# Side transfers of weight sums on ScalarE's queue, seven raw buffers for output tiles, and packed rows of scale and bias in a fox/RWKV-7 layer

## The chip, the cores and the metric

The kernel runs on one core of a Trainium2 chip. The time is device microseconds of one execution, and the numbers compared are medians of several. The engines of the core are TensorE (PE in profiles, its weight loads PEld), VectorE (DVE), ScalarE (ACT), GpSimd (POOL) and SyncE (SP). Each runs its own list of instructions in order; semaphores make one wait for another. A DMA is issued by an instruction on an engine's queue and is carried out by 16 DMA engines.

## The reference, cut to what matters

```python
proj = einsum('bsd,dc->bsc', x, w_in)            # 256 x 4096 by 4096 x 16592
fox_out  = fox_attention(q, k, v, log_sigmoid(f + f_bias))        # 16 heads of 128
rwkv_out = groupnorm(rwkv7_scan(r, decay, k, v, -kk, kk * a)) + bonus   # 32 heads of 64
h   = concat(fox_out, rwkv_out) * silu(z)
out = einsum('bsc,cd->bsd', h, w_out)            # 256 x 4096 by 4096 x 4096
x   = layernorm(ALPHA * x + out, ln_gain, ln_bias)
```

## The kernel before, in words

All products are made in float32r: a weight tile is split into a rounded half (ScalarE, L153) and the rest (VectorE, L154), and TensorE sums three products of halves. A raw weight tile is 128 x 1024 float32 (two rows of 128 inputs by 512 columns, 512 KB), loaded by SyncE in `load` (L252) into a ring of four buffers. `fetch` (L258) keeps up to three loads ahead of the split, and `weights` (L276) up to three split tiles ahead of TensorE. A full tile is used in 12 matmuls of 512 columns.

The program has two halves. **The projection** goes over eight pairs of head groups (n), four blocks (b) of 512 columns each and 16 tiles (q) a block. After every second group of three matmuls it calls `slot` (L212), which lets each of a list of generators (`sides`) issue its next step; `wait(n)` in a generator passes n slots. The generators do everything that is not projection: attention, the RWKV-7 scan in chunks, transposes through DRAM (`bt`, `vt`), gates, and the weight sums.

**The output projection** has eight blocks of 512 columns. For blocks 3/4 and 5/6 and eight of the 16 tiles (`FEW`), a scheme of the Strassen kind saves products. It needs four combinations of four weight tiles b11, b12, b21, b22, two from each block of the pair. They are made ahead, during the projection, by `weight_sums` (L833): two loads of 512 KB from `w_o` into `ts`, four subtractions on GpSimd (L842), one store of 1 MB to DRAM (`td`). There is one `ts` buffer, and 16 sums in all. In the output stage a tile of FEW is a group of four jobs: e1 (a tile of w_o, 6 matmuls), e2 (half a tile, 3), e3 and e4 (halves of `td`, 6 each). The other tiles are plain jobs ("n") of 12. `plan` (L221 to 229) writes the order of the jobs down; `stream` and `jobs` follow it, so the loads stand in SyncE's queue in this order too. Between jobs, `drain` issues pending VectorE work (`todo`) of blocks done before.

`load_tok` (L932) loads the residual and the rows of scale and bias for a block: it makes three-term splits of them in six partitions of `rows` (128 x 4096, zero elsewhere). At the end `moments` (L1248) computes the layer norm's factors; they are written into six columns of a zeroed 128 x 128 tile, transposed by TensorE, and multiplied with `rows` (L1311, L1348), which gives the outer products of the norm with scale and bias.

Names in profiles: `w` and `wo` are raw tiles, with h and l behind them the halves; `e` the raw tiles of e1 to e4; `acc`, `oacc`, `p` PSUM accumulators; `ts` and `td` the sums.

Of the kernel before, what the change touches and what calls it, by code (L numbers as in the profile page):

```python
# [92 lines left out]
def layer(ctx: ExitStack, tc: tile.TileContext, xt, xtok, w_main, w_lora, w_first, muv, w_o, up, par, mulora, fbias, lng, lnb, cst, out):  # L93
# [156 lines left out]
    raws = {}  # L250

    def load():  # L252
        name, src = stream.pop()
        raw = wpool.tile([P, 1024], F32, tag="wr", name=name, bufs=4)
        nc.sync.dma_start(out=raw[:, : src.shape[1] * OB], in_=src.rearrange("p k c -> p (k c)"))
# [577 lines left out]
    def weight_sums():  # L833
        g = nc.gpsimd.tensor_tensor
        for b, q in tds:
            t = rp.tile([P, 4, OB], F32, tag="ts", name=f"ts{b}_{q}")
            for n in range(2):
                issue(t[:, 2 * n : 2 * n + 2], w_o[b + n][:, 2 * q : 2 * q + 2, :])
            yield from wait(6)
            b11, b21, b12, b22 = (t[:, n] for n in range(4))  # L840
            for o, x, y in ((b11, b12, b11), (b12, b22, b12), (b22, b22, b11), (b21, b21, b22)):
                g(o, x, y, ALU.subtract)  # L842
# [89 lines left out]
    def load_tok(b):  # L932
# [5 lines left out]
        rr = rpool.tile([6, OB], F32, tag="rr", name=f"rr{b}")  # L938
        nc.sync.dma_start(out=rr[0:3], in_=lng[:, o].to_broadcast([3, OB]))
        nc.sync.dma_start(out=rr[3:6], in_=lnb[:, o].to_broadcast([3, OB]))  # L940
        rh = rpool.tile([6, OB], F32R, tag="rh", name=f"rh{b}")
        nc.scalar.copy(rh, rr)
        rt_ = rpool.tile([6, OB], F32, tag="rt", name=f"rt{b}")
        nc.vector.tensor_scalar(rt_, rh.bitcast(F32), cs[0:6, C_ROW : C_ROW + 1], None, ALU.mult)
        nc.vector.scalar_tensor_tensor(rows[0:6, o], rr, cs[0:6, C_ROW + 1 : C_ROW + 2], rt_, ALU.mult, ALU.add)
# [220 lines left out]
    whole = len(FEW) * 5 + LEAD  # L1166
    for kind, b, q in plan:
# [51 lines left out]
        if b == 0 and q == KT // 2 - 1:  # L1219
# [5 lines left out]
            rows = rpool.tile([P, D], F32R, name="rows")  # L1225
# [21 lines left out]

    def moments(m):  # L1248
# [6 lines left out]
        nc.gpsimd.memset(z[:, 3:5], 1.0)  # L1255
# [6 lines left out]
        if m:  # L1262
            h = [rpool.tile([P, 1], F32R, name=f"zah{n}") for n in range(2)]
            nc.gpsimd.tensor_copy(h[0], mean)  # L1264
            nc.gpsimd.tensor_copy(za[:, 0:3:2], h[0].bitcast(F32).to_broadcast([P, 2]))
            nc.gpsimd.tensor_tensor(za[:, 1:2], mean, h[0].bitcast(F32), ALU.subtract)
            nc.scalar.copy(h[1], sd)
            nc.scalar.copy(za[:, 3:5], h[1].bitcast(F32).to_broadcast([P, 2]))
            nc.scalar.activation(za[:, 5:6], h[1].bitcast(F32), AF.Identity, scale=-1.0, bias=sd)
# [76 lines left out]
    def other(n):  # L1346
        o = slice(n * OB, (n + 1) * OB)
        nc.tensor.matmul(wps[n], la, rows[:, o], start=False, stop=True)  # L1348
# [64 lines left out]
```

## Time and profile before

| | |
|---|---|
| runs | 1958.45, 1960.71, 1960.96 us; median 1960.71 |
| profiled execution | 1960.14 us, its span 1958.4 us |
| TensorE, VectorE, ScalarE, GpSimd busy | 98%, 76%, 52%, 18% of the span |
| DMA | 466.74 MB, mean 238 GB/s |

The busy share of TensorE counts a matmul from its start to a modelled end, and ends overlap the next start; the distance between starts is the better measure of pace. A row of the table by stages has the stretch, its length, and for each engine its busy time with the number of instructions, then the granted TensorE clock, the share of time in which the DMA engines were busy, and GB/s. "A <- B: t, n, m" in the waits is A waiting for B, t us in total, n times, at most m.

### The profile page before, as it was taken

To read this page: it belongs to the slowest core of one execution; us is meant where nothing else is said; L and a number is where in the kernel's file an instruction comes from. 1 tells how busy PE (TensorE), PEld (TensorE's weight loads), DVE (VectorE), ACT (ScalarE), POOL (GpSimd) and SP (SyncE) were. 2 spreads that over 40 slices of the span, in tenths; PEclk is the share of its full clock that TensorE was granted. 3 is DMA by queue.
4 is the path that set the end of the run, shared out by engine and by line. 5 is a ranking of instruction groups with operands and counts; after the bars stand their busy time and mean duration, and the time that the engine had idled before them with its cause. 6 is when DMAs were issued, how large, how long until landed. Compare 5 with 4: busy or idle time off the path is not lost.

```text
span 1958.4 us, 28349 instructions
## 1 busy us (share of the span) xinstructions
PE 1915.0 (98%) x9745; PEld 1574.4 (80%) x9745; DVE 1484.7 (76%) x2469; ACT 1012.2 (52%) x1581; POOL 361.9 (18%) x530
## 2 busy tenths in 40 slices
PE   9999999999999999999999999999999999998998
PEld 9888787778787888788888888888888878866766
DVE  7688868786878687868776877778677856966667
ACT  6544555455535653555446454645564554554543
POOL 0233223222332142212200220131013001000000
PEclk9999999999999999999999999999999999999999
DMA  9678877886897788777776687677777876777784
GB/s 345 193 249 265 256 229 255 270 250 195 276 278 241 228 284 263 239 215 242 228 224 195 209 243 215 199 224 231 206 218 217 301 221 211 224 255 244 262 263 168
DMA packets 281348, 466.74 MB, mean 238 GB/s; under 512 B 143666, under 2 KB 170948, under 8 KB 279156
## 3 DMA queue, kind: packets, MB, share of 16 engines
q1 hardware_dynamic: 280916, 464.59, 76.3%
q8 instruction: 76, 1.25, 0.3%
q14 instruction: 68, 0.56, 0.1%
q10 hardware_dynamic: 288, 0.34, 0.1%
HBM read 418.43 MB, written 46.42 MB: 237 GB/s over the span
## 4 chain that ended last, share of the span: by engine, by line
PE 81%; DVE 7%; DMA 7%; ACT 2%; SPq 1%; issue 1%; DVEq 0%; ACTq 0%; POOL 0%
PE acc L161 21%; PE acc L159 21%; PE acc L160 20%; PE oacc L963 4%; PE oacc L960 4%; PE oacc L961 4%; DMA e<-td 2%; DMA w<-in_w_main_dram 2%; DMA e<-in_w_o_dram 1%; SPq L318 1%; PE rh L691 1%; PE gp L577 1%; DVE prod L644 1%; PE up L722 1%; PE sp L732 1%
## 5 line engine op out<-in xcount | busy, mean ns | idle before, releaser
L806 POOL COPY pT<-lg 32x96 f32<-32x96 f32 x128 | 58.3, 456 | 419.7 <-DVE lg L802 414.9
L842 POOL TENSOR_TENSOR ts<-ts 128x512 f32<-128x512 f32 x64 | 100.4, 1568 | 182.9 <-DMA ts<-in_w_o_dram 177.6
L614 POOL COPY BKt<-BK 32x192 f32<-32x192 f32 x128 | 73.2, 572 | 60.8 <-DVE BK L611 55.8
L644 DVE TENSOR_TENSOR prod<-Nb,xc 128x8 f32<-128x8 f32 (+30 forms) x248 | 78.1, 315 | 2.9
L647 DVE TENSOR_REDUCE xc<-prod 128x8 f32<-128x16 f32 (+30 forms) x248 | 72.5, 292 | 6.6
L154 DVE TENSOR_TENSOR w_0l<-w,w_0h 128x1024 fp32r<-128x1024 f32 x31 | 37.9, 1222 | 36.5 <-ACT w_0h L153 25.4
L153 ACT CAST w_0h<-w 128x1024 fp32r<-128x1024 f32 x31 | 32.5, 1047 | 55.3 <-DMA w<-in_w_main_dram 41.4
L153 ACT CAST w_6h<-w 128x1024 fp32r<-128x1024 f32 x31 | 32.7, 1055 | 50.0 <-PE acc L160 27.0
L1264 POOL CAST zah<-mv 128x1 fp32r<-128x1 f32 x1 | 0.2, 188 | 305.9 <-DVE mv L1259 305.9
L154 DVE TENSOR_TENSOR w_11l<-w,w_11h 128x1024 fp32r<-128x1024 f32 x31 | 39.8, 1284 | 21.9 <-ACT w_11h L153 11.6
L154 DVE TENSOR_TENSOR w_7l<-w,w_7h 128x1024 fp32r<-128x1024 f32 x31 | 40.4, 1305 | 19.3 <-ACT w_7h L153 8.6
L154 DVE TENSOR_TENSOR w_10l<-w,w_10h 128x1024 fp32r<-128x1024 f32 x31 | 38.8, 1251 | 20.3 <-ACT w_10h L153 12.2
L503 POOL COPY hr<-hr 32x16 f32<-32x16 f32 x64 | 38.4, 600 | 78.6 <-DVE hr L500 76.2
L153 ACT CAST w_8h<-w 128x1024 fp32r<-128x1024 f32 x31 | 32.6, 1051 | 37.5 <-DMA w<-in_w_main_dram 20.6
L161 PE MATMUL acc<-w_11l,x 128*128 128x512 f32 x124 | 47.6, 397 | 4.1 <-DVE w_11l L154 4.1
L154 DVE TENSOR_TENSOR w_8l<-w,w_8h 128x1024 fp32r<-128x1024 f32 x31 | 40.8, 1317 | 14.3 <-ACT w_8h L153 10.5
L787 POOL TENSOR_SCALAR_AFFINE_SELECT nb<-nb 128x128 f32<-128x128 f32 x32 | 22.7, 716 | 153.5 <-DMA nb<-ncd 93.5
L159 PE MATMUL acc<-w_9h,x 128*128 128x512 f32 x124 | 50.1, 404 | 0.8 <-ACT w_9h L153 0.8
L154 DVE TENSOR_TENSOR w_6l<-w,w_6h 128x1024 fp32r<-128x1024 f32 x31 | 38.9, 1254 | 15.6 <-PE acc L161 7.5
L159 PE MATMUL acc<-w_10h,x 128*128 128x512 f32 x124 | 49.6, 400 | 1.0 <-ACT w_10h L153 1.0
L161 PE MATMUL acc<-w_12l,x 128*128 128x512 f32 x124 | 48.1, 392 | 2.2 <-DVE w_12l L154 2.2
L154 DVE TENSOR_TENSOR w_15l<-w,w_15h 128x1024 fp32r<-128x1024 f32 x31 | 38.5, 1242 | 15.3 <-issue 13.1
(1052 smaller groups left out, 6845.8 us busy)
## 6 DMA issues: line engine op xcount, KB each, us to landing
w<-in_w_main_dram SPq DMA_DIRECT2D x496, 512.0 KB
wo<-in_w_o_dram SPq DMA_DIRECT2D x96, 512.0 KB
ts<-in_w_o_dram SPq DMA_DIRECT2D x32, 512.0 KB
td<-ts SPq DMA_DIRECT2D x16, 1024.0 KB
e<-td SPq DMA_DIRECT2D x32, 512.0 KB
bt<-bk SPq DMA_DIRECT2D x88, 128.0 KB
Nb<-nd SPq DMA_DIRECT2D x16, 512.0 KB
e<-in_w_o_dram SPq DMA_DIRECT2D x16, 512.0 KB
```

What stands on the lines that cost most here:

```text
L153: latest[1] = nc.scalar.copy(hi[:, :n], src[:, :n])
L154: latest[0] = nc.vector.tensor_tensor(lo[:, :n], src[:, :n], hi[:, :n].bitcast(F32), ALU.subtract)
L159: nc.tensor.matmul(acc[:, :n], xs[k][:, 0, tt], hi[:, o : o + n], start=(k == 0), stop=False)
L160: nc.tensor.matmul(acc[:, :n], xs[k][:, 1, tt], hi[:, o : o + n], start=False, stop=False)
L161: nc.tensor.matmul(acc[:, :n], xs[k][:, 0, tt], lo[:, o : o + n], start=False, stop=(k == KT - 1))
L614: nc.gpsimd.tensor_copy(BKt[B * b : B * (b + 1), :, :, B * a : B * (a + 1)], BK[B * a : B * (a + 1), :, : NCH - 1, B * b : B * (b + 1)])
L644: first = nc.vector.tensor_tensor(prod[:, :, :, s + 1 :], nb[:, :, s : s + 1, s + 1 :].to_broadcast([P, 2, NJ, w]), xc[:, :, :, s + 1 :], ...
L647: solved = nc.vector.tensor_reduce(xc[:, :, :, s : s + 1], prod[:, :, :, s:], AX.X, ALU.add)
L842: g(o, x, y, ALU.subtract)
L960: nc.tensor.matmul(acc, h, hi, start=n[0] == n[1], stop=False)
L961: nc.tensor.matmul(acc, l, hi, start=False, stop=False)
L963: nc.tensor.matmul(acc, h, lo, start=False, stop=not n[0])
```

## The change

It has three parts.

1. `weight_sums` issues its DMAs on ScalarE's queue instead of SyncE's: four loads of 256 KB, two slots apart, and two stores of 512 KB, five slots apart, instead of two loads of 512 KB and one store of 1 MB. The four subtractions are issued six slots apart instead of two.
2. In the output stage, once the memory of the projection is free (`rpool` exists), raw tiles come from two rings, four and three buffers, and up to six loads run ahead instead of three. In the stretches of e jobs the plain jobs are spread over all of it: three stand ahead and three at the end (`LEAD`, `TAIL`), and the ten others go among the groups, mostly one to a group, two for the fourth and the eighth.
3. `rows` is 128 x 2 x 512 instead of 128 x 4096: block b lies in partitions 32 (b mod 4) and following, column group b // 4. The factors are written into four groups of columns at once, and the last matmuls take 32 partitions.

```diff
-LEAD = 4
+LEAD = 3
+TAIL = 3
-REST = 13
+RING = (4, 3)
...
+        at = LEAD
         for n, q in enumerate(FEW):
-            plan += [("e1", b, q), ("e2", b, q), plain[LEAD + n], ("e3", b, q), ("e4", b, q)]
-        plan += plain[LEAD + len(FEW) :]
+            to = LEAD + (len(plain) - LEAD - TAIL) * (n + 1) // len(FEW)
+            plan += [("e1", b, q), ("e2", b, q)] + plain[at : at + 1] + [("e3", b, q), ("e4", b, q)] + plain[at + 1 : to]
+            at = to
+        plan += plain[at:]
...
-        raw = wpool.tile([P, 1024], F32, tag="wr", name=name, bufs=4)
+        wide = rpool is not None
+        turn_of[0] = (turn_of[0] + 1) % (sum(RING) if wide else RING[0])
+        own = turn_of[0] >= RING[0]
+        raw = (rpool if own else wpool).tile([P, 1024], F32, tag="we" if own else "wr", name=name, bufs=RING[own])
...
-        while len(raws) < 3 and stream:
+        while len(raws) < (3 if rpool is None else sum(RING) - 1) and stream:
...
+        def send(out, src):
+            tc.keep_in_program_order(nc.scalar.dma_start(out=out, in_=src))
+
         for b, q in tds:
             t = rp.tile([P, 4, OB], F32, tag="ts", name=f"ts{b}_{q}")
-            for n in range(2):
-                issue(t[:, 2 * n : 2 * n + 2], w_o[b + n][:, 2 * q : 2 * q + 2, :])
+            for n in range(4):
+                send(t[:, n], w_o[b + n // 2][:, 2 * q + n % 2, :])
+                yield from wait(2)
             yield from wait(6)
             b11, b21, b12, b22 = (t[:, n] for n in range(4))
             for o, x, y in ((b11, b12, b11), (b12, b22, b12), (b22, b22, b11), (b21, b21, b22)):
                 g(o, x, y, ALU.subtract)
-                yield from wait(2)
-            yield from wait(REST)
-            issue(tds[b, q], t)
+                yield from wait(6)
             yield from wait(6)
+            for n in (2, 0):
+                send(tds[b, q][:, n : n + 2], t[:, n : n + 2])
+                yield from wait(5)
...
-        rr = rpool.tile([6, OB], F32, tag="rr", name=f"rr{b}")
+        a = slice(32 * (b % 4), 32 * (b % 4) + 6)
+        rr = rpool.tile([P, OB], F32, tag="rr", name=f"rr{b}")
...
+    def outer(acc, l, b, **flags):
+        a = slice(32 * (b % 4), 32 * (b % 4 + 1))
+        nc.tensor.matmul(acc, l[a], rows[a, b // 4, :], **flags)
...
-    whole = len(FEW) * 5 + LEAD
+    whole = KT + 2 * len(FEW) - TAIL
...
-            rows = rpool.tile([P, D], F32R, name="rows")
+            rows = rpool.tile([P, 2, OB], F32R, name="rows")
...
-        nc.tensor.matmul(wp, l, rows[:, o], start=True, stop=True)
+        outer(wp, l, b, start=True, stop=True)
```

SyncE's queue in pair 1, block 3 of the projection, before (w1_3_7 is tile 7 of that block, ts3_10 the sum for blocks 3/4 and tile 10, bt1_2 a transposed block on its way through DRAM):

```order
L255 DMA w1_3_4_3616<-in_w_main_dram 128x1024
L318 DMA td3_9_845<-ts3_9_3296 128x2048
L255 DMA w1_3_5_3645<-in_w_main_dram 128x1024
L255 DMA w1_3_6_3669<-in_w_main_dram 128x1024
L255 DMA w1_3_7_3698<-in_w_main_dram 128x1024
L318 DMA bt1_2_3685<-bk1_2_3611 64x16x32 x4
L318 DMA ts3_10_3712<-in_w_o_dram 128x1024 x2
L318 DMA vt1_3723<-UV1_3477 64x8x32
L318 DMA fq2_3725<-bt1_2_3685 128x256
L318 DMA fk2_3726<-bt1_2_3685 128x256
L255 DMA w1_3_8_3731<-in_w_main_dram 128x1024
```

The same place on SyncE after the change:

```order
L264 DMA w1_3_4_3610<-in_w_main_dram 128x1024
L264 DMA w1_3_5_3638<-in_w_main_dram 128x1024
L264 DMA w1_3_6_3663<-in_w_main_dram 128x1024
L264 DMA w1_3_7_3692<-in_w_main_dram 128x1024
L327 DMA bt1_2_3679<-bk1_2_3605 64x16x32 x4
L327 DMA vt1_3714<-UV1_3469 64x8x32
L264 DMA w1_3_8_3722<-in_w_main_dram 128x1024
```

The store td3_9 and the loads ts3_10 are gone from the queue. They stand on ScalarE now, one pair later since the sums go on more slowly, between the casts of raw tiles:

```order
L155 CAST w2_2_15h_5395<-w2_2_15_5338 128x1024
L846 DMA td3_9_845<-ts3_9_4806 128x1024
L155 CAST w2_3_0h_5414<-w2_3_0_5375 128x1024
L155 CAST w2_3_1h_5432<-w2_3_1_5393 128x1024
L846 DMA td3_9_845<-ts3_9_4806 128x1024
...
L155 CAST w2_3_4h_5508<-w2_3_4_5454 128x1024
L846 DMA ts3_10_5522<-in_w_o_dram 128x512
L155 CAST w2_3_5h_5539<-w2_3_5_5482 128x1024
L846 DMA ts3_10_5522<-in_w_o_dram 128x512
L155 CAST w2_3_6h_5570<-w2_3_6_5506 128x1024
```

Each cast behind such a DMA waits until the DMA could be issued. On GpSimd, around this sum before (BKt and pT are copies for the scan and for attention):

```order
L614 COPY BKt1_3514<-BK1_3043 32x6x32 x16
L842 TENSOR_TENSOR ts3_10_3712<-ts3_10_3712 128x512 x4
L806 COPY pT2_3931<-lg2_3862 32x3x32 x8
L787 AFFINE_SELECT nb3_4447<-nb3_4447 128x128 x2
L842 TENSOR_TENSOR ts3_11_4171<-ts3_11_4171 128x512 x4
```

And around it on GpSimd after the change:

```order
L623 COPY BKt2_5350<-BK2_4882 32x6x32 x16
L856 TENSOR_TENSOR ts3_10_5522<-ts3_10_5522 128x512 x4
L815 COPY pT4_5767<-lg4_5698 32x3x32 x8
L796 AFFINE_SELECT nb5_6280<-nb5_6280 128x128 x2
L856 TENSOR_TENSOR ts3_11_6307<-ts3_11_6307 128x512
L815 COPY pT5_6428<-lg5_6342 32x3x32 x8
```

The four subtractions of tile 10 still stand together; of tile 11, one has come to stand ahead of the pT copies and three behind them. In the output stage the jobs are read off ScalarE's casts. On ScalarE before, in blocks 3/4 at tiles 7 and 8 (e33_7 is job e3 for block 3, tile 7):

```order
L153 CAST e13_7h_16682<-e13_7_16653 128x1024
L153 CAST e23_7h_16694<-e23_7_16662 128x512
L153 CAST wo3_15h_16706<-wo3_15_16680 128x1024
L153 CAST e33_7h_16718<-e33_7_16692 128x1024
L153 CAST e43_7h_16727<-e43_7_16704 128x1024
L153 CAST e13_8h_16745<-e13_8_16716 128x1024
L153 CAST e23_8h_16757<-e23_8_16725 128x512
```

The same place on ScalarE after the change:

```order
L155 CAST e13_7h_16718<-e13_7_16641 128x1024
L155 CAST e23_7h_16730<-e23_7_16653 128x512
L155 CAST wo3_14h_16742<-wo3_14_16665 128x1024
L155 CAST e33_7h_16754<-e33_7_16689 128x1024
L155 CAST e43_7h_16763<-e43_7_16698 128x1024
L155 CAST wo3_15h_16781<-wo3_15_16716 128x1024
L155 CAST e13_8h_16793<-e13_8_16728 128x1024
```

A second plain job, wo3_15, has come between e4 of tile 7 and e1 of tile 8.

More of the change, by code (lines that the diff above doesn't have):

```diff
@@ L86, in constants @@
     sign = np.array([-1, -1, -1, 1, 1, 1], np.float32)
-    cst[:6, C_ROW] = sign * (2 * first - 1)
-    cst[:6, C_ROW + 1] = sign * (1 - first)
+    for a in range(0, P, 32):
+        cst[a : a + 6, C_ROW] = sign * (2 * first - 1)
+        cst[a : a + 6, C_ROW + 1] = sign * (1 - first)
     return cst
@@ L250, in layer @@
     raws = {}
+    turn_of = [0]
     def load():
         name, src = stream.pop()
-        raw = wpool.tile([P, 1024], F32, tag="wr", name=name, bufs=4)
+        wide = rpool is not None
+        turn_of[0] = (turn_of[0] + 1) % (sum(RING) if wide else RING[0])
+        own = turn_of[0] >= RING[0]
+        raw = (rpool if own else wpool).tile([P, 1024], F32, tag="we" if own else "wr", name=name, bufs=RING[own])
         nc.sync.dma_start(out=raw[:, : src.shape[1] * OB], in_=src.rearrange("p k c -> p (k c)"))
@@ L937, in load_tok @@
         nc.sync.dma_start(out=lgain[b], in_=lng[:, o].to_broadcast([P, OB]))
-        rr = rpool.tile([6, OB], F32, tag="rr", name=f"rr{b}")
[L939 to L945, printed above, removed]
+        a = slice(32 * (b % 4), 32 * (b % 4) + 6)
+        rr = rpool.tile([P, OB], F32, tag="rr", name=f"rr{b}")
+        nc.sync.dma_start(out=rr[a.start : a.start + 3], in_=lng[:, o].to_broadcast([3, OB]))
+        nc.sync.dma_start(out=rr[a.start + 3 : a.stop], in_=lnb[:, o].to_broadcast([3, OB]))
+        rh = rpool.tile([P, OB], F32R, tag="rh", name=f"rh{b}")
+        nc.scalar.copy(rh[a], rr[a])
+        rt_ = rpool.tile([P, OB], F32, tag="rt", name=f"rt{b}")
+        nc.vector.tensor_scalar(rt_[a], rh[a].bitcast(F32), cs[a, C_ROW : C_ROW + 1], None, ALU.mult)
+        nc.vector.scalar_tensor_tensor(rows[a, b // 4, :], rr[a], cs[a, C_ROW + 1 : C_ROW + 2], rt_[a], ALU.mult, ALU.add)
+    def outer(acc, l, b, **flags):
+        a = slice(32 * (b % 4), 32 * (b % 4 + 1))
+        nc.tensor.matmul(acc, l[a], rows[a, b // 4, :], **flags)
     def part(t, j):
@@ L1246, in factors, with four, spread4 @@
         return z
+    def four(z):
+        return z.rearrange("p (a c) -> p a c", c=32)
+    def spread4(v, n):
+        return v.unsqueeze(2).to_broadcast([P, 4, n])
     def moments(m):
@@ L1254, in moments @@
         z = factors(m, "d")
-        nc.gpsimd.memset(z[:, 3:5], 1.0)
+        nc.gpsimd.memset(four(z)[:, :, 3:5], 1.0)
         za = factors(m, "a") if m else None
@@ L1264, in moments @@
             nc.gpsimd.tensor_copy(h[0], mean)
-            nc.gpsimd.tensor_copy(za[:, 0:3:2], h[0].bitcast(F32).to_broadcast([P, 2]))
-            nc.gpsimd.tensor_tensor(za[:, 1:2], mean, h[0].bitcast(F32), ALU.subtract)
+            nc.gpsimd.tensor_copy(four(za)[:, :, 0:3:2], spread4(h[0].bitcast(F32), 2))
+            nc.gpsimd.tensor_tensor(four(za)[:, :, 1:2], spread4(mean, 1), spread4(h[0].bitcast(F32), 1), ALU.subtract)
             nc.scalar.copy(h[1], sd)
-            nc.scalar.copy(za[:, 3:5], h[1].bitcast(F32).to_broadcast([P, 2]))
-            nc.scalar.activation(za[:, 5:6], h[1].bitcast(F32), AF.Identity, scale=-1.0, bias=sd)
+            nc.scalar.copy(four(za)[:, :, 3:5], spread4(h[1].bitcast(F32), 2))
+            nc.scalar.activation(four(za)[:, :, 5:6], spread4(h[1].bitcast(F32), 1), AF.Identity, scale=-1.0, bias=sd)
             deviation(0, mean)
@@ L1276, in moments @@
         pin(nc.vector.tensor_copy(zh, s2))
-        pin(nc.vector.tensor_copy(z[:, 0:3:2], zh.bitcast(F32).to_broadcast([P, 2])))
-        last = pin(nc.vector.tensor_tensor(z[:, 1:2], s2, zh.bitcast(F32), ALU.subtract))
+        pin(nc.vector.tensor_copy(four(z)[:, :, 0:3:2], spread4(zh.bitcast(F32), 2)))
+        last = pin(nc.vector.tensor_tensor(four(z)[:, :, 1:2], spread4(s2, 1), spread4(zh.bitcast(F32), 1), ALU.subtract))
         if m:
@@ L1347, in other @@
         o = slice(n * OB, (n + 1) * OB)
-        nc.tensor.matmul(wps[n], la, rows[:, o], start=False, stop=True)
+        outer(wps[n], la, n, start=False, stop=True)
         nc.scalar.mul(res[1][:, o], wps[n], rss[1])
```

## The prediction

> **What bounds the kernel now.** I read the page's first part, then the table by stages, then the rows of single stalls.
>
> ```profile
> span 1958.4 us, 28349 instructions
> PE 1915.0 (98%) x9745; PEld 1574.4 (80%) x9745; DVE 1484.7 (76%) x2469; ACT 1012.2 (52%) x1581; POOL 361.9 (18%) x530
> ```
>
> TensorE is the bound nearly everywhere, so only time in which it stands still can be won. The table by stages shows where that is. Its first seven stages each run from one head pair's first gp matmul to the next pair's, the last two are the stretches with the e jobs (side products) of blocks 3/4 and 5/6:
>
> ```profile
> core 0: us, PE busy (x) PEld busy (x) DVE busy (x) ACT busy (x) POOL busy (x), PEclk, DMA share, GB/s
> 143.05:339.32 196.27, 192.07 (x1004) 157.04 (x1004) 159.20 (x268) 103.27 (x167) 57.22 (x74) 1.00 0.81 250
> 339.32:538.10 198.78, 193.74 (x1003) 158.06 (x1002) 154.47 (x258) 100.22 (x164) 58.38 (x72) 0.99 0.79 249
> 538.10:732.87 194.77, 192.19 (x1002) 158.44 (x1002) 150.08 (x258) 100.19 (x164) 53.48 (x71) 0.99 0.83 257
> 732.87:926.68 193.81, 191.12 (x1003) 157.20 (x1002) 150.29 (x258) 101.58 (x165) 48.01 (x66) 1.00 0.78 240
> 926.68:1116.35 189.67, 189.67 (x1002) 157.59 (x1002) 145.82 (x257) 101.58 (x164) 31.69 (x56) 1.00 0.74 218
> 1116.35:1306.03 189.68, 189.68 (x1003) 157.59 (x1002) 145.46 (x257) 101.68 (x164) 32.74 (x56) 1.00 0.74 217
> 1306.03:1495.70 189.67, 189.67 (x1002) 157.58 (x1002) 145.18 (x257) 101.60 (x164) 32.13 (x55) 1.00 0.74 216
> 1716.14:1790.47 74.33, 64.20 (x261) 47.00 (x259) 43.05 (x40) 36.74 (x39) 0.00 (x0) 1.00 0.76 254
> 1814.79:1888.23 73.44, 66.58 (x266) 49.24 (x265) 44.89 (x42) 37.20 (x39) 0.00 (x0) 0.98 0.79 261
> ```
>
> The same thousand matmuls take 189.67 us in three later stages and more in the four before: 6.60 + 9.11 + 5.10 + 4.14 = 24.95 us over. What differs is the weight sums, by tile:
>
> ```profile
> L842 POOL TENSOR_TENSOR ts<-ts x64: 1285/1326/2326, 74.3 to 832.2; 128x512 f32<-128x512 f32 x64
> L318 SPq DMA_DIRECT2D ts<-in_w_o_dram x32: 327/428/1053, 67.2 to 819.6; - x32
> L318 SPq DMA_DIRECT2D td<-ts x16: 382/424/617, 110.5 to 871.9; - x16
> ```
>
> They end at 872 us, and with them the loss. The last two stages hold 8 x 33 = 264 matmuls each. TensorE's pace without a wait, first and thirteenth matmul of a row of 12:
>
> ```profile
> 1702.54 0.39 PE L960 MATMUL oacc<-wo_15h,hl 128*128 128x512 f32 x1
> ...
> 1705.26 0.39 PE L960 MATMUL oacc<-wo_0h,h 128*128 128x512 f32 x1
> ```
>
> That is 2.72/12 = 0.2267 us, so 59.85 us for 264; the stretches lose 74.33 - 59.85 = 14.48 and 73.44 - 59.85 = 13.59, together 28.1 us. These two sums, 25.0 and 28.1, are what the change can work on.
>
> **Seven raw buffers and the new order of jobs.** In the first e stretch SyncE, which issues the loads, stands before loads whose buffer VectorE has not yet freed; its waits there, of which I quote three (total, times, longest), and the chain of one load:
>
> ```profile
> SPq L255 <- DVE e_5l L154: 7.3, 4, 3.5
> SPq L255 <- DVE e_10l L154: 6.4, 4, 2.4
> SPq L255 <- DVE e_11l L154: 6.0, 4, 2.4
> ```
> ```profile
> 1732.33 6.18 DMA e<-td
> 1738.61 1.05 ACT e_6h L153
> 1739.69 1.24 DVE e_6l L154
> ```
>
> A buffer is thus held 6.18 + 1.05 + 1.24 = about 8.5 us, and four can't keep up with jobs as short as 3 to 12 matmuls. It is the buffers and not the DMA engines that limit: one step (e1, e2, a plain job, e3, e4) loads 2.36 MB, and at full pace lasts 33 x 0.2267 = 7.48 us, which needs 315 GB/s. Got are 254, at a DMA share of 0.76. The rows of more load are
>
> ```profile
> 30.00:32.00 2.00, 2.00 (x14) 2.00 (x14) 1.25 (x3) 0.75 (x2) 0.00 (x0) 1.00 1.04 413
> 1735.00:1740.00 5.00, 3.93 (x16) 2.66 (x15) 1.54 (x2) 2.25 (x3) 0.00 (x0) 1.00 1.00 363
> ```
>
> so 315 lies within what was reached. Three more buffers are 1.57 MB, 4.3 us at 363 GB/s: more than the longest wait for a free buffer, 3.5 us. What is late next is VectorE: 4 x 1.24 for full tiles and half of that for e2 make 5.6 us of each 7.48, so it keeps up, if without much room for the merges. Nine plain jobs instead of eight stand among the e jobs now; each loads 0.52 MB for 2.72 us of matmul (193 GB/s), which eases the stretch further. I leave 1.5 us of loss in each of the two: gain 28.1 - 3 = **25.1 us**; bounds 0 (the rate, not the buffers, binds) and 28.1.
>
> **Weight sums: slower, in pieces, on ScalarE's queue.** One sum took 6 + 8 + 13 + 6 = 33 slots, now 8 + 6 + 24 + 6 + 10 = 54. Stores now 50.8 us apart ((871.9 - 110.5)/15) will be about 83 us apart, and the last falls near 1450 us, still before the output stage that reads it. So the three clean stages get sums too, some 2.2 each where the bad ones had 3.9. Two things cause the loss now. One is SyncE's queue, here ahead of the stall at 384 us:
>
> ```profile
> 358.46 0.43 SPq L318 DMA_DIRECT2D td<-ts  x1
> 359.38 4.34 SPq L255 DMA_DIRECT2D w<-in_w_main_dram  x3
> 364.79 6.58 SPq L318 DMA_DIRECT2D bt<-bk  x4
> 371.41 1.18 SPq L318 DMA_DIRECT2D ts<-in_w_o_dram  x2
> ```
>
> Behind the 1 MB store the four bt transfers take 6.58 us to issue, then come two ts loads of 512 KB, and only then w loads. That part leaves the queue. The other cause is VectorE held up by GpSimd's four subtractions in a row, ahead of the stall at 483 us:
>
> ```profile
> 477.40 6.40 POOL L842 TENSOR_TENSOR ts<-ts 128x512 f32<-128x512 f32 x4 [7.30 <-DMA ts<-in_w_o_dram]
> ```
> ```profile
> 477.96 1.81 DVE L154 TENSOR_TENSOR w_7l<-w,w_7h 128x1024 fp32r<-128x1024 f32 x1 [0.53 <-ACT w_7h L153]
> 479.70 1.52 DVE L770 TENSOR_TENSOR post<-post 128x256 f32<-128x256 f32 x1
> 481.25 1.40 DVE L771 TENSOR_TENSOR post<-post,bon 128x256 f32<-128x256 f32 x1
> 482.57 2.30 DVE L154 TENSOR_TENSOR w_8l<-w,w_8h 128x1024 fp32r<-128x1024 f32 x1
> ...
> 485.92 1.21 DVE L154 TENSOR_TENSOR w_9l<-w,w_9h 128x1024 fp32r<-128x1024 f32 x1
> ```
>
> w_8l takes 2.30 us in the burst, w_9l 1.21 after it. The 64 subtractions stay, and in the new order the four of a sum mostly still stand together; only the staggered pieces set the first apart. I give half of the 25 us to each cause, take the first as gone but for 2 us, the second as falling from 12.5 to 8 since w loads come in time more often: 10 us stay, gain **15 us**; bounds 25 and, if later stages lose as the early ones did, 0. The Trainium skill ("SBUF — State Buffer", Who interferes with whom) says that a VectorE instruction with two SBUF inputs and a GpSimd one that reads SBUF lock each other out for a whole instruction; the rows above agree, and it speaks for the first rival below.
>
> ScalarE gets 16 x 6 = 96 sends. It has issued two in this trace, and SyncE waited for a store of sums:
>
> ```profile
> L130 ACTq DMA_DIRECT2D lr<-in_w_lora_dram x2: 407/430/453, 0.7 to 1.2; - x2
> ```
> ```profile
> SPq L318 <- DMA td<-ts: 9.0, 5, 5.2
> ```
>
> 96 x 0.43 = 41 us in all, 6 per stage on top of 102 busy of 190: hidden by idle time. New are the waits: a send queued behind a semaphore holds the w casts behind it, and VectorE and TensorE wait for those. The first ts piece waits for the store before it, at worst 9.0 us in all as SyncE did; the td sends wait for GpSimd, 12 slots (18 us) after the last subtraction. Up to three split jobs of 2.72 us are ready ahead, so a wait under 8 us is mostly covered. I charge **2 us**, bounds 0 and 9. The Trainium skill ("DMA: Bandwidth & Descriptors", Issuing engines are not separate DMA queues) holds that a second issuing queue adds no bandwidth, only issue time. By it the queue's half would stay and the sum come to 1932.5; the bt row above, whose issue took 6.58 us behind a store, speaks against it, and no run here shows side transfers on a second queue.
>
> **Packed rows.** They make the room for the three buffers. The last matmuls use 32 rows and stream the same 512 columns; factors are written four times, at the end in the chain:
>
> ```profile
> 1947.21 0.19 ACT za L1268
> 1949.01 0.70 PE wp L1348 x3
> ```
>
> No row shows the new forms; by these neighbours a few hundredths of a us each, between -0.2 and +0.4 in all; I take 0.
>
> **The sum.** The profiled execution took 1960.1 us (span 1958.4), 0.6 below the median of the runs. 1960.1 - 25.1 - 15 + 2 = 1922.0; as a median 1922.6.
>
> **Rivals.**
> - *The subtractions keep the first loss.* VectorE's loss by bursts is only spread over more stages. For it: busy time of VectorE is 150 where the sums run, 145 where not, and that work is unchanged. Against: several bursts in the bad stages cost TensorE nothing. 1960.1 - 25.1 + 2 = 1937. Chance 0.18. It is what the rule on the shared reads would give if every stall came that way.
> - *The bytes and not the queue hold up the w loads.* The sums' pieces take the DMA engines' time wherever they are issued, so the 10.5 us that I put down to SyncE's queue stay, thinned over more stages. For it: a DMA share of 0.78 to 0.83 with the sums and 0.74 without. Against: engines that are free a fifth of the time. 1960.1 - 25.1 - 4.5 + 2 = 1932.5. Chance 0.10. It is what the rule on issuing queues would give.
> - *Rate and not buffers binds the e jobs.* For it: the two e stretches both got 254 to 261 GB/s. Against: the 363 and 413 rows. 1960.1 - 15 + 2 = 1947. Chance 0.12. With the first rival too, 1962, no change: 0.04.
> - *Slower: ScalarE held by its sends.* A ts piece or td send waits with w casts queued behind it, once in each of the 16 sums; from more than 40/16 = 2.5 us of TensorE standstill per sum it eats both gains. At 5 us: 1960.1 - 25 - 15 + 80 = 2000. For it: SyncE's longest wait of 5.2 us for such a store. Against: the ready jobs, and five waits in 16. Chance 0.06.
> - *It doesn't do what it says:* the loads don't run ahead since they wait for something else in SyncE's order. That is the third rival's time, and in its chance.
>
> **How the numbers follow.** My forecast has 0.50. Over 0.2% (4 us) is what a measurement can tell here. Faster: 0.50 + 0.18 + 0.10 + 0.12 = 0.90; same 0.04; slower 0.06. With both losses gone wholly the time is 1960.1 - 53 = 1907. The range, 1908 to 1948, goes from there to the third rival.
>
> **What would show it.** Right: the two e stretches (now with nine plain jobs, 276 matmuls, 62.6 us) within 2 us of that; all seven pair stages between 190 and 193 us; no wait of ScalarE over 5 us before a cast that follows a send. Wrong: DMA share near 1.0 with TensorE idle in the e stretches (rate), VectorE rows of 2 us beside GpSimd's with stages of 194 us and more (subtractions), ScalarE idle before casts with the raw tile landed (sends).

## The result, and the profile after

The changed kernel takes 1930.26 us (median of 4 runs, 1927.99 to 1932.55), the kernel before 1959.58 in runs beside it. The ratio is 0.9856, 95% interval 0.9833 to 0.9879: 1.4% faster. The profiled execution took 1930.38 us. That is inside the range and 7.7 us above the forecast.

The first part of the page of the changed kernel:

```profile
span 1928.6 us, 28470 instructions
PE 1905.0 (99%) x9745; PEld 1574.9 (82%) x9745; DVE 1489.4 (77%) x2469; ACT 1012.8 (53%) x1581; POOL 356.9 (19%) x530
```

The number of matmuls is the same and nearly all of the span is TensorE's again. Next, its table by stages: the seven pair stages, the two stretches of e jobs (now 276 matmuls each), the sum over the seven pair stages alone, and the part from the last pair's first gp matmul to the end, after and before.

```profile
141.32:339.26 197.94, 193.43 (x1005) 158.79 (x1004) 156.50 (x268) 103.03 (x167) 52.68 (x70) 0.99 0.78 234
339.26:534.03 194.77, 192.21 (x1003) 158.59 (x1002) 153.36 (x258) 101.20 (x164) 40.92 (x64) 0.99 0.77 237
...
918.81:1110.43 191.62, 190.83 (x1002) 157.15 (x1002) 150.78 (x257) 101.26 (x165) 44.67 (x64) 1.00 0.79 240
1110.43:1300.29 189.86, 189.86 (x1002) 157.47 (x1002) 151.47 (x257) 101.13 (x164) 48.45 (x66) 1.00 0.80 248
1300.29:1489.96 189.67, 189.67 (x1002) 157.59 (x1002) 145.68 (x257) 101.64 (x164) 34.78 (x58) 1.00 0.76 224
1708.83:1773.48 64.65, 63.70 (x277) 51.76 (x276) 47.69 (x45) 39.67 (x43) 0.00 (x0) 1.00 0.91 313
1792.53:1855.94 63.41, 63.41 (x278) 51.84 (x276) 49.32 (x47) 39.69 (x43) 0.00 (x0) 1.00 0.92 320
sum 1348.64, PE 1336.79 PEld 1104.29 DVE 1057.30 ACT 710.59 POOL 316.06; mean PE 190.97 PEld 157.75 DVE 151.04 ACT 101.51 POOL 45.15
1489.96:1928.60 438.64, 428.46 (x2022) 346.78 (x2022) 333.39 (x499) 221.48 (x297) 21.09 (x48) 0.99 0.75 251
```
```profile
1495.70:1958.40 462.70, 436.94 (x2022) 346.93 (x2022) 331.64 (x499) 221.04 (x297) 23.58 (x48) 0.99 0.73 238
```

The last part is 24.1 us shorter (462.70 to 438.64). The pair stages are only 4.0 shorter: seven times 189.67 is 1327.69, so 20.95 us of standstill are left of 24.95. The last pair starts 5.74 us earlier (1489.96, before 1495.70), of which the missing 1.7 were won ahead of the first stage. 24.1 + 5.7 is the whole of it. The stretches of e jobs run at 313 and 320 GB/s, within 2.1 and 0.8 us of the 62.6 that their matmuls need. So the time that is missing against the forecast is missing in the projection. There ScalarE waits longer for a late first w tile of a block (total, times, longest) than the 41.4 us, 10 times, of before:

```profile
ACT w_0h L155 <- DMA w<-in_w_main_dram: 57.7, 14, 8.4
```

Two further places are worth a look, one in the projection and one near the end. First, VectorE and GpSimd around 910 us (vs is other work of GpSimd, hr a small copy on GpSimd that VectorE needs):

```profile
897.85 2.94 POOL L856 TENSOR_TENSOR ts<-ts 128x512 f32<-128x512 f32 x2 [12.44 <-DMA ts<-in_w_o_dram]
...
899.57 2.94 DVE L554 TENSOR_TENSOR BK<-k,eI 64x256 f32<-64x256 f32 x2
...
902.55 2.21 DVE L156 TENSOR_TENSOR w_5l<-w,w_5h 128x1024 fp32r<-128x1024 f32 x1
904.68 2.30 DVE L156 TENSOR_TENSOR w_6l<-w,w_6h 128x1024 fp32r<-128x1024 f32 x1
905.86 2.27 POOL L856 TENSOR_TENSOR ts<-ts 128x512 f32<-128x512 f32 x1
908.09 1.29 POOL L592 TENSOR_TENSOR vs<-vs,bk 128x512 f32<-128x512 f32 x1
909.44 0.89 POOL L512 COPY hr<-hr 32x16 f32<-32x16 f32 x4
910.36 0.17 DVE L556 TENSOR_TENSOR hr<-hr 128x16 f32<-128x16 f32 x1 [3.38 <-POOL hr L512]
...
910.90 1.21 DVE L156 TENSOR_TENSOR w_7l<-w,w_7h 128x1024 fp32r<-128x1024 f32 x1
```

While GpSimd is at work, a low part takes 2.2 to 2.3 us instead of 1.21, and TensorE waits 1.00 us for w_5l. Then VectorE stands 3.38 us for hr, which is queued behind four subtractions and three vs operations; w_7l comes behind that wait, and TensorE stands another 1.63 us for it. The wait for hr looks like the work of the subtractions, but experiment 2 finds it without them.

The other place is new. TensorE and its weight loads, where the rows of scale and bias enter (wp), with 32 rows now, and the same place before with 128:

```profile
1907.91 0.40 PE L983 MATMUL oacc<-wo,h 128*128 128x512 f32 x1
1908.23 0.18 PEld L965 LDWEIGHTS wp<-rows,l 32*128 32x128 f32 x1 [0.37 <-issue]
1908.23 0.50 PE L965 MATMUL wp<-rows,l 32*128 32x512 f32 x1
1908.66 0.19 PEld L980 LDWEIGHTS oacc<-wo_13h,h 128*128 128x128 f32 x1 [0.24 <-issue]
1908.66 0.50 PE L980 MATMUL oacc<-wo_13h,h 128*128 128x512 f32 x1
...
1909.00 0.39 PE L981 MATMUL oacc<-wo_13h,h 128*128 128x512 f32 x1
```
```profile
1939.65 0.39 PE L963 MATMUL oacc<-wo,h 128*128 128x512 f32 x1
1939.65 0.19 PEld L1311 LDWEIGHTS wp<-rows,l 128*128 128x128 f32 x1
1939.88 0.39 PE L1311 MATMUL wp<-rows,l 128*128 128x512 f32 x1
```

Before, each start follows the last by 0.23 us, and the weights of wp are loaded from the start of the matmul ahead on. Now 0.32, 0.43 and 0.34 us pass around a wp, since neither its weights nor the next matmul's are loaded until 0.1 us before the (modelled) end of the matmul ahead. From the transpose ahead of these matmuls to the last product it takes 11.11 us instead of 7.99: 3.1 us for eight, 0.39 each.

### The profile page after: what moved, and what is told of

It is laid out like the page before. It is cut to its first block, busy times and chain, and to the rows that moved or that the text cites. A ratio compares the mean times of both kernels' runs of the same rounds, so it can differ in the third digit from the quotient of the medians.

```text
span 1928.6 us, 28470 instructions
## 1 busy us (share of the span) xinstructions
PE 1905.0 (99%) x9745; PEld 1574.9 (82%) x9745; DVE 1489.4 (77%) x2469; ACT 1012.8 (53%) x1581; POOL 356.9 (19%) x530
## 4 chain that ended last, share of the span: by engine, by line
PE 90%; DVE 5%; DMA 2%; ACT 1%; issue 1%; SPq 0%; DVEq 0%; POOL 0%; ACTq 0%; POOLq 0%
PE acc L161 22%; PE acc L163 22%; PE acc L162 22%; PE oacc L980 4%; PE oacc L983 4%; PE oacc L981 4%; DMA w<-in_w_main_dram 1%; PE rh L700 1%; PE p L980 1%; PE p L983 1%; PE p L981 1%; PE gp L586 1%; PE up L731 1%; PE sp L741 1%; DVE prod L653 1%
## 5 line engine op out<-in xcount | busy, mean ns | idle before, releaser
L653 DVE TENSOR_TENSOR prod<-Nb,xc 128x8 f32<-128x8 f32 (+30 forms) x248 | 83.4, 336 | 3.0
L155 ACT CAST w_0h<-w 128x1024 fp32r<-128x1024 f32 x31 | 32.5, 1048 | 64.5 <-DMA w<-in_w_main_dram 57.7
L156 DVE TENSOR_TENSOR w_9l<-w,w_9h 128x1024 fp32r<-128x1024 f32 x31 | 39.1, 1260 | 19.6 <-ACT w_9h L155 8.7
L156 DVE TENSOR_TENSOR w_6l<-w,w_6h 128x1024 fp32r<-128x1024 f32 x31 | 43.0, 1387 | 13.3 <-ACT hry L774 7.3
L155 ACT CAST w_10h<-w 128x1024 fp32r<-128x1024 f32 x31 | 32.6, 1052 | 35.1 <-DMA w<-in_w_main_dram 27.1
L161 PE MATMUL acc<-w_0h,x 128*128 128x512 f32 x124 | 49.9, 403 | 1.1 <-ACT bk L1114 1.0
L163 PE MATMUL acc<-w_5l,x 128*128 128x512 f32 x124 | 48.7, 392 | 1.6 <-DVE w_5l L156 1.6
L155 ACT CAST w_1h<-w 128x1024 fp32r<-128x1024 f32 x31 | 32.7, 1054 | 33.4 <-DMA w<-in_w_main_dram 15.7
L161 PE MATMUL acc<-w_15h,x 128*128 128x512 f32 x124 | 50.1, 404 | 0.0
L155 ACT CAST w_9h<-w 128x1024 fp32r<-128x1024 f32 x31 | 32.6, 1050 | 33.3 <-DMA w<-in_w_main_dram 17.6
```

What stands on the lines that cost most here:

```text
L155: latest[1] = nc.scalar.copy(hi[:, :n], src[:, :n])
L156: latest[0] = nc.vector.tensor_tensor(lo[:, :n], src[:, :n], hi[:, :n].bitcast(F32), ALU.subtract)
L161: nc.tensor.matmul(acc[:, :n], xs[k][:, 0, tt], hi[:, o : o + n], start=(k == 0), stop=False)
L163: nc.tensor.matmul(acc[:, :n], xs[k][:, 0, tt], lo[:, o : o + n], start=False, stop=(k == KT - 1))
L653: first = nc.vector.tensor_tensor(prod[:, :, :, s + 1 :], nb[:, :, s : s + 1, s + 1 :].to_broadcast([P, 2, NJ, w]), xc[:, :, :, s + 1 :], ...
```

## Experiments

After the traces the theories for the 20.95 us that stay in the projection were: S, the subtractions hold up VectorE; B, the bytes of the sums' transfers make the w loads late; Q, the queue that issues them matters, SyncE's or now ScalarE's; and that the loss isn't the sums' at all.

**1. No sums.** It leaves out the sums' transfers and subtractions; e3 and e4 jobs read w_o.

```
-        return tds[b, q][:, 2:4] if kind == "e3" else tds[b, q][:, 0:2]
+        return w_o[b + (kind == "e3")][:, two, :]
...
     def weight_sums():
+        yield
```

> The changed kernel without the sums' transfers and subtractions (the e3 and e4 jobs read w_o in place of the sums). It says how much of the 20.95 us that seven pair stages of the changed kernel spend beyond 189.67 us belongs to the sums at all. If they cause it, as all theories of the prediction take it, each stage is 189.7 to 190.5 and the time 1930.3 - 19 = about 1911. If the first stages lose for another reason, the first two keep most of their 8.3 and 5.1 us: about 1922.

Measured: 1910.94 us (1910.32 to 1911.21). Its stages, the first and the sum over all seven, and ScalarE's wait for the first w tile of each block (total, times, longest):

```profile
140.63:332.94 192.31, 190.92 (x1004) 157.56 (x1004) 150.63 (x268) 104.04 (x167) 35.54 (x58) 1.00 0.71 214
...
sum 1330.44, PE 1329.05 PEld 1103.00 DVE 1023.63 ACT 714.06 POOL 225.42; mean PE 189.86 PEld 157.57 DVE 146.23 ACT 102.01 POOL 32.20
```
```profile
ACT w_0h L155 <- DMA w<-in_w_main_dram: 27.7, 6, 6.5
```

Without sums 2.75 us of loss stay (1330.44 - 1327.69), 2.64 of it in the first stage. The sums cost the changed kernel 18.2 us in its stages and 19.3 in its time.

**2. No subtractions.** All transfers are kept, the 64 subtractions are left out (the stored tiles are raw weights).

```
-                g(o, x, y, ALU.subtract)
```

> The changed kernel with all transfers of the sums and none of the 64 subtractions (the stored tiles are raw weights). Theory S (the subtractions hold up VectorE): nearly the time without any sums, 1911 to 1914. Theory B (bytes or queue of the transfers hold up the w loads): no change, 1928 to 1931.

Measured: 1918.01 us (1917.41 to 1918.29).

```profile
sum 1336.14, PE 1331.29 PEld 1102.51 DVE 1020.97 ACT 711.03 POOL 215.94; mean PE 190.18 PEld 157.50 DVE 145.85 ACT 101.58 POOL 30.85
```
```profile
ACT w_0h L155 <- DMA w<-in_w_main_dram: 43.5, 11, 8.0
```

Between both expectations: 12.3 us go with the subtractions, and 8.45 - 2.75 = 5.7 us of loss stay with transfers alone. ScalarE's waits for the late first tile are 43.5 us against 27.7 without transfers. At the place that stood at 910 us in the changed kernel, the wait for hr is there without any subtraction, behind the same three vs operations:

```profile
897.81 0.17 DVE L556 TENSOR_TENSOR hr<-hr 128x16 f32<-128x16 f32 x1 [3.51 <-POOL hr L512]
```

TensorE does not stand there now. So that wait by itself fits into the tiles that are split ahead. That the longer low parts ahead of it, and loads that came late, had used them up in the changed kernel is argued from the rows.

**3. No transfers.** Subtractions on a tile of zeros, with nothing sent; e3 and e4 read w_o.

```
+        nc.gpsimd.memset(t, 0.0)
         for b, q in tds:
-            for n in range(4):
-                send(t[:, n], w_o[b + n // 2][:, 2 * q + n % 2, :])
-                yield from wait(2)
-            yield from wait(6)
+            yield from wait(14)
```

> The changed kernel with the 64 subtractions at the same slots, on a tile of zeros, and without the sums' transfers. Theory S: as the changed kernel, 1927 to 1931. Theory B: nearly the time without any sums, 1911 to 1914.

Measured: 1966.21 us (1962.71 to 1967.43), outside both expectations. It does not answer the question: with no data to wait for, the 64 subtractions stand nearly in a row in GpSimd's order, from 71 us to 178. But it is the clearest view of what one does to VectorE. The stretch of the burst, then GpSimd and VectorE in it:

```profile
71.50:178.50 107.00, 67.78 (x255) 52.83 (x254) 83.77 (x63) 31.91 (x50) 103.04 (x70) 0.79 0.38 114
```
```profile
99.64 13.48 POOL L850 TENSOR_TENSOR ts<-ts 128x512 f32<-128x512 f32 x9
...
101.20 1.51 DVE L538 TENSOR_TENSOR k<-s,am 128x256 f32<-128x256 f32 x1
...
105.47 1.48 DVE L554 TENSOR_TENSOR BK<-k,eI 64x256 f32<-64x256 f32 x1
...
106.88 0.69 DVE L507 STREAM_TRANSPOSE hq<-sb 128x512 f32<-128x512 f32 x1
...
108.40 0.69 DVE L509 TENSOR_REDUCE hr<-hq 128x16 f32<-128x512 f32 x1
```

One subtraction takes 13.48/9 = 1.50 us, and so do the VectorE instructions with two inputs from SBUF that stand in a row, whatever they need alone (the BK of 64x256, 1.48 us here, takes 0.43 in the changed kernel at 495 us). They take turns with the subtractions, one for one. The transpose and the reduction, with one input, take 0.69 us here, and 0.71 and 0.68 in the changed kernel at 895 and 897 us. This agrees with the Trainium skill ("SBUF — State Buffer", Who interferes with whom), by which a VectorE instruction with two SBUF inputs and a GpSimd one that reads SBUF contend for an exclusive lock. TensorE got only 255 matmuls done in 107 us.

**4. The small pieces through SyncE.** The queue alone undone.

```
-            tc.keep_in_program_order(nc.scalar.dma_start(out=out, in_=src))
+            issue(out, src)
```

> The changed kernel with its small pieces issued by SyncE, in the same slots, instead of ScalarE: the queue alone undone. The prediction put half of the loss to SyncE's queue: then some 10 us slower, 1940. If the queue doesn't matter and only bytes or subtractions do: 1929 to 1932. If ScalarE is held by its sends now: faster, 1922 to 1927.

Measured: 1929.22 us (1927.70 to 1931.84). The seven stages:

```profile
sum 1347.28, PE 1335.21 PEld 1101.77 DVE 1055.60 ACT 709.29 POOL 321.35; mean PE 190.74 PEld 157.40 DVE 150.80 ACT 101.33 POOL 45.91
```

No difference that shows, 19.59 us of loss in place of 20.95. For these small pieces theory Q falls: it doesn't matter which of the two queues issues them, and ScalarE wasn't held by its sends either. The large pieces of before were not run on ScalarE's queue, so whether the queue mattered for them stays open.

**5. The sums as before.** Output stage as changed, the sums in large pieces on SyncE, done by 870 us.

```
-            for n in range(4):
-                send(t[:, n], w_o[b + n // 2][:, 2 * q + n % 2, :])
-                yield from wait(2)
+            for n in range(2):
+                issue(t[:, 2 * n : 2 * n + 2], w_o[b + n][:, 2 * q : 2 * q + 2, :])
...
-                yield from wait(6)
+                yield from wait(2)
+            yield from wait(REST)
+            issue(tds[b, q], t)
```

> The changed kernel with the sums of the kernel before: 512 KB pieces through SyncE, the four subtractions close together, done by 870 us; buffers, order of jobs and packed rows as changed. By the two traces the output part alone gives 24.1 us and the new way of the sums 4.0 (24.96 less 20.94 us of loss): 1934. By the prediction's terms (25.1 and 15 less 2) it is 1930.3 + 13 = 1943.

Measured: 1935.76 us (1933.68 to 1938.30), ratio to the kernel before 0.9879 (0.9865 to 0.9893). The new way of the sums is worth 5.5 us by the medians, and the two kernels' runs do not overlap; by the stages it is 25.63 - 20.95 = 4.7 (its seven take 1353.32 us). The forecast has 13.

**6. Thin transfers.** All 96 transfers at their places, each cut to 64 B of every 2 KB, and all subtractions, on one tile of zeros; e3 and e4 read w_o.

```
-                send(t[:, n], w_o[b + n // 2][:, 2 * q + n % 2, :])
+                send(t[:, n, 0:16], w_o[b + n // 2][:, 2 * q + n % 2, 0:16])
...
-                send(tds[b, q][:, n : n + 2], t[:, n : n + 2])
+                send(tds[b, q][:, n : n + 2, 0:16], t[:, n : n + 2, 0:16])
```

> The changed kernel with the sums' 96 transfers at the same places, each cut to 64 B of every 2 KB, and all 64 subtractions (on a tile of zeros; e3 and e4 read w_o). Only the bytes go. Theory S, subtractions cost most of the 19.3 us that the kernel without sums saves: no_subtract has shown transfers alone to cost 7, so 1923 to 1925. Rival, the two costs don't add and the bytes make late loads that make the subtractions hurt: 1915. If the sends and their waits cost and not the bytes: 1929 to 1931.

Measured: 1918.55 us (1917.80 to 1921.14).

```profile
sum 1335.81, PE 1331.08 PEld 1102.47 DVE 1053.83 ACT 711.21 POOL 322.03; mean PE 190.15 PEld 157.50 DVE 150.55 ACT 101.60 POOL 46.00
```

The bytes alone are worth 11.7 us. Subtractions alone leave 8.12 - 2.75 = 5.4 us of loss, transfers alone 5.7, both together 18.2: 7.1 more than the sum. By the medians of the runs, against the kernel without sums, they cost 7.6 and 7.1 us alone and 19.3 together, still 4.6 more than the sum. So neither S nor B is the whole answer: each by itself mostly stays within the three jobs that are split ahead, and together they exceed them. (That it is this slack which they share is argued from the rows; no run changed the slack.) It is not that the subtractions come in shorter rows here: in 9 of the 16 sums all four run with no pause of 1 us between them, in 8 in the changed kernel. VectorE's busy time in the stages stays at 1053.83, near the 1057.30 of the changed kernel: its longer instructions cost TensorE little while loads come in time.

**7. Subtractions apart.** Pieces in another order and at other slots, so that the subtractions come as one, two and one.

```
+            for n in (0, 2):
+                send(t[:, n], w_o[b + n // 2][:, 2 * q + n % 2, :])
+                yield from wait(2)
+            yield from wait(12)
+            g(b11, b12, b11, ALU.subtract)
+            for n in (3, 1):
+                send(t[:, n], w_o[b + n // 2][:, 2 * q + n % 2, :])
+                yield from wait(14)
...
-                yield from wait(5)
+                yield from wait(2)
```

> The changed kernel with a sum's pieces sent at other slots, so that the subtractions come as 1, 2 and 1 with some 20 us between them, instead of mostly four in a row; same transfers, same number of slots. If a stall needs several subtractions in a row, most of the 12.3 us that the subtractions cost goes: 1919 to 1923. If each subtraction costs its share wherever it stands (0.19 us): no change, 1929 to 1931.

Measured: 1927.47 us (1927.30 to 1928.05), ratio 0.9837 (0.9823 to 0.9850): 2.8 us below the changed kernel, with intervals that overlap. The sum of the stages, and the one that lost most:

```profile
1101.52:1297.68 196.16, 193.02 (x1002) 159.34 (x1002) 151.49 (x257) 100.91 (x164) 45.30 (x65) 0.98 0.78 238
sum 1346.95, PE 1336.99 PEld 1105.28 DVE 1057.87 ACT 709.37 POOL 318.94; mean PE 191.00 PEld 157.90 DVE 151.12 ACT 101.34 POOL 45.56
```

6.49 of its 19.26 us lie in one stage. ScalarE there, and TensorE behind it:

```profile
1123.28 0.34 ACTq L846 DMA_DIRECT2D ts<-in_w_o_dram  x1
1123.74 1.04 ACT L155 CAST w_2h<-w 128x1024 fp32r<-128x1024 f32 x1 [2.81 <-DMA td<-ts]
...
1125.91 0.79 PE L161 MATMUL acc<-w_0h,x 128*128 128x512 f32 x1 [3.14 <-ACT bk L1119]
```

The next sum's first send, only two slots behind the store that has to land first, held ScalarE 2.81 us, and TensorE stood 3.14. This is the mechanism of the slower rival, made by closing up the slots. The granted clock fell behind that standstill, which cost some 2.4 us more (last section). Without that stage 12.8 us of loss would be left; whether spacing alone gives that stays open.

**8. Full rows again.** The eight wp matmuls of row half 0 with 128 rows, on the packed rows: four factor tiles of zeros, each filled in one group of 32.

```
+    l0 = [rpool.tile([P, P], F32R, name=f"l0{a}") for a in range(4)]
...
+            for a in range(4):
+                at = slice(32 * a, 32 * a + 32)
+                tc.keep_in_program_order(nc.scalar.copy(l0[a][at], zp[at, :P]))
...
+            nc.tensor.matmul(wp, l, rows[:, b // 4, :], start=True, stop=True)
```

> The changed kernel, but the eight matmuls that end row half 0 use all 128 rows again (four factor tiles, each with one group of 32 rows filled, on the packed rows). In the changed kernel the part from the transpose ahead of them to the last product takes 11.11 us, before it took 7.99. If the change between 32 and 128 rows costs this: 8.0 us again and 3.1 us faster, 1927. If it is something else (banks, VectorE): 11 us and no change.

Measured: 1928.79 us (1925.66 to 1935.52). The part that the edit touches:

```profile
1906.97 0.27 PE L1358 MATMUL zp<-cs,zd 128*128 128x128 f32 x1
...
1914.91 0.39 PE L983 MATMUL oacc<-wo_15l,hl 128*128 128x512 f32 x1
```
```profile
1491.79:1927.70 435.91, 425.67 (x2022) 347.56 (x2022) 333.51 (x499) 222.22 (x300) 22.37 (x52) 0.99 0.75 253
```

From the transpose to the last product it takes 7.94 us, against 11.11 in the changed kernel and 7.99 before, and the last part 435.91 in place of 438.64. The change between 32 and 128 rows costs the 3.1 us. The whole time can't show it alone, since the projection of this run lost 2.3 us more.

**9. Halved subtractions.** Each as two of 256 columns.

```
+                for c in (slice(0, OB // 2), slice(OB // 2, OB)):
+                    g(o[:, c], x[:, c], y[:, c], ALU.subtract)
```

> The changed kernel with each subtraction as two of 256 columns (128 in all), at the same places. If VectorE waits for a whole GpSimd instruction at a time, the cast's low part in a burst takes some 1.2 + 0.7 = 1.9 us in place of 2.3, and the 12.3 us that the subtractions cost fall to 6 to 9: 1924 to 1927. Rival: the burst only gets longer, and VectorE waits for GpSimd's own work that is queued behind it (the head sums): no gain or a loss, 1929 to 1936.

Measured: 1929.63 us (1927.48 to 1935.17): no change. The stages' sum:

```profile
sum 1346.35, PE 1335.38 PEld 1104.53 DVE 1043.95 ACT 710.72 POOL 338.14; mean PE 190.77 PEld 157.79 DVE 149.14 ACT 101.53 POOL 48.31
```

VectorE's busy time falls by 13 us (1057.30 to 1043.95) and GpSimd's grows by 22. At the place that stood at 910 us VectorE waits 5.46 us for hr in place of 3.38, and TensorE 3.10 in place of 1.63, as the rival said. In all VectorE's waits for hr are 11.9 us against 5.0, but they are 7.3 without any subtraction, so this total alone shows little. A shorter lock is not a shorter burst.

**10 and 11. The order of jobs without the buffers, and the buffers without the order.**

```
-RING = (4, 3)
+RING = (4, 0)
```
```
-LEAD = 3
-TAIL = 3
+LEAD = 4
...
+            plan += [("e1", b, q), ("e2", b, q), plain[LEAD + n], ("e3", b, q), ("e4", b, q)]
+        plan += plain[LEAD + len(FEW) :]
```

> The changed kernel with four raw buffers in the output stage too, three loaded ahead: the new order of jobs alone. If the buffers did it, as the prediction says, each stretch of e jobs still loses 10 us or more, and the part after the last gp matmul takes 458 to 466 us in place of 438.7: 1950 to 1958. If the new order with its ninth plain job did it: 1931 to 1936.

> The changed kernel with the order of jobs before (one plain job in each step, four ahead) and seven buffers: the buffers alone. If the buffers did it: 1930 to 1934. If the rate limits a step with one plain job (315 GB/s wanted): the stretches lose 5 us or more each and the time is 1940 or more.

Measured: 1951.52 us (1949.90 to 1956.22) with four buffers, 1931.45 (1930.44 to 1934.98) with seven and the old order. The last parts of the two:

```profile
1495.24:1954.40 459.16, 439.17 (x2022) 345.23 (x2022) 333.15 (x499) 222.09 (x297) 21.62 (x48) 0.99 0.74 240
```
```profile
1492.04:1929.90 437.86, 428.48 (x2022) 346.97 (x2022) 333.25 (x499) 221.67 (x297) 20.96 (x48) 0.99 0.76 252
```

The first of the two stretches of e jobs with the old order, 264 matmuls that need 59.85 us:

```profile
1713.64:1774.33 60.69, 60.69 (x266) 49.58 (x264) 45.20 (x42) 38.68 (x42) 0.00 (x0) 1.00 0.94 323
```

The buffers did it: 437.86 with them alone, and the stretch runs within 0.9 us of its matmuls at 323 GB/s. The new order gives nothing once they are there. With four buffers it gives some 6.6 us: 459.16, against 462.70 before plus the 3.1 of the packed rows.

These two kernels, that of experiment 8 and the changed kernel share the code of the projection. Their profiled executions lost 25.2 (four buffers, its slowest run), 22.0, 23.3 and 20.95 us in the seven stages. So the stages of a single execution scatter by some 4 us, and differences in projection loss between the changed kernel and experiments 4, 7, 9 and 12 (18.7 to 23.3) show nothing. The 18.2 us of the sums stand clear of it; the 4.7 of experiment 5 do not, and rest on the runs.

**12. Both edits that took time off.** The diffs of 7 and 8 together.

> The changed kernel with both edits that took time off: the subtractions 1, 2, 1 apart and the eight matmuls of half 0 on 128 rows. If they add, 1930.3 - 2.8 - 2.7 = 1924.8, faster than both kernels; the part after the last gp matmul takes 435.5 to 436.5 us. If the gain of the spread subtractions was only scatter: 1927 to 1928.

Measured: 1925.07 us (1922.42 to 1928.56), ratio 0.9838 (0.9819 to 0.9857). It is the shortest median of the versions with the whole computation, but the kernel before was faster beside it too (1957.07), and the ratio is that of experiment 7 (0.9837).

```profile
sum 1350.95, PE 1337.72 PEld 1105.66 DVE 1056.91 ACT 709.53 POOL 320.86; mean PE 191.10 PEld 157.95 DVE 150.99 ACT 101.36 POOL 45.84
1491.86:1926.50 434.64, 425.33 (x2023) 347.46 (x2022) 333.30 (x499) 222.33 (x300) 21.49 (x52) 0.99 0.74 253
```

The last part, 434.64, keeps the gain of the full rows. The stages lost 23.3 us in its profiled execution, the wait behind the store among them again, so the gain of the spread subtractions is not shown.

## Why the prediction was right or wrong

- **Output stage, 25.1 us: right.** The stretches themselves fell from 28.1 us of loss to 2.9, a gain of 25.1 us. The runs give it to the buffers, as argued: the last part takes 437.86 us with buffers alone, 459.16 with the order alone. The load that I worked out as needed, 315 GB/s, is what the stretches now get (313 and 320, and 323 with the old order), so the rival by which the rate binds is refuted. VectorE kept up. That the whole last part shows 24.1 is partly luck: the plain jobs between the stretches won some 2.5 us that I had not counted, and the packed rows took 3.1. Of the signs, the first stretch misses its 2 us by a hair (2.1).
- **Weight sums, 15 us less 2: the step that failed.** 5.7 came. "I give half of the 25 us to each cause, take the first as gone but for 2 us": moving the pieces off SyncE's queue is worth nothing that shows (1929.22 with all small pieces back on it). The bt row on which I put it was one of the two longest: over the 22 groups of four bt transfers the issue takes 3.8 us in the median before, and 3.4 in the kernel without sums. What the transfers do cost comes from their bytes, on either queue, and mostly together with the subtractions. The gain that there is comes with smaller pieces, spread over seven stages; no run parted size from spacing, or tried large pieces on ScalarE's queue. The Trainium skill's rule ("DMA: Bandwidth & Descriptors", Issuing engines are not separate DMA queues) had this right for the small pieces. The time that I gave by it, 1932.5, was nearer, but that is partly luck: it adds up two costs that do not add.
- **The subtractions "from 12.5 to 8".** Taking them away gives 12.3 of the changed kernel's time, so that cost is all there. "Since w loads come in time more often" fails too: ScalarE's waits for the first tile of a block grew from 41.4 to 57.7 us. The first two rivals described one half each; neither alone gives the measured 20.95 us.
- **"The three clean stages get sums too, some 2.2 each".** They lost 1.95, 0.19 and nothing, though the first two of them had at least two sums each, as many as the second stage, which lost 5.1. The last had only the end of one: the stores did come some 81 us apart, but 110.5 + 15 x 83 is 1355.5 and not the 1450 that I wrote, and the last store went out at 1353.7. "All seven pair stages between 190 and 193" fails in the first two, 197.94 and 194.77, and in the last two, which are shorter. 2.6 of the first stage's 8.3 us stay without any sums.
- **ScalarE's sends, 2 us: nothing.** The same pieces on SyncE take the same time. Two casts behind sends waited over 5 us (8.3 and 8.4), but by the profile for their own raw tile. The slower rival was rightly small: its mechanism appeared only where experiment 7 put a send two slots behind a store.
- **Packed rows, 0, bounds -0.2 to +0.4: outside the bounds, 3.1 us.** I priced the new matmuls by rows of matmuls with 128 rows; that eight of them would stand singly between such neighbours is what I left out. The Trainium skill has the rule that I should have weighed ("TensorEngine Tiling (Array Packing)", Key Properties): changing the tiling mode drains TensorE. It gives no price; here it is 0.39 us for a matmul of 32 rows between others of 128.

In sum: 1960.1 - 24.1 - 5.7 = 1930.3.

## What to carry to other kernels

Two numbers tell beforehand whether more buffers pay: how long a load holds its buffer, and how many loads full pace needs in that time. Here five loads in 7.48 us, each holding a buffer for some 8.5, make 5.7 buffers by estimate; four fell short and seven did. The rate that this needs has to be within reach too. Before a side job's cost is divided among causes, take each cause away alone and then all: here two causes that leave 5.4 and 5.7 us alone made 18.2 together, and the third, the queue, showed nothing. Profile the same code more than once before a few microseconds of one trace are given a cause. A matmul of fewer rows is not free because its columns are the same; among full ones, filling its rows with zeros was cheaper.

## What the runs showed of the hardware that was not expected

- A 32-row matmul among 128-row ones costs 0.39 us beyond its place: the weight loads on either side of it start only in the last 0.1 us of the matmul ahead, by its modelled end.
- VectorE with two SBUF inputs and GpSimd take turns, one instruction each: 1.51 us for a 128x256 operation beside subtractions of 1.50, while transposes and reductions are untouched (0.69 us). Start to start a turn is 1.40 to 1.44 us, less than 1.28 and 0.42 together (the shortest subtraction of the changed kernel, and such an operation there at 894 us, with no subtraction beside it). So they do not exclude each other for all of their recorded time.
- A standstill costs more than its length. After the 3.14 us in experiment 7 the granted clock fell, and twelve matmuls came 0.43 us apart instead of 0.23, some 2.4 us more:

```profile
1126.00:1130.00 4.00, 4.00 (x10) 3.13 (x11) 1.73 (x6) 2.33 (x3) 1.28 (x1) 0.50 0.57 190
```
